# Opening of a diffusion-step kernel: PSUM banks by name, vec first on SyncE's queue, one gate product and two modulation products moved

## The chip, the cores and the metric

The kernel runs on one core of one Trainium2 chip. The metric is device microseconds of one execution, lower is better, as the median of three runs.

## The reference, cut to what matters

One layer of a hybrid backbone over 512 latent tokens ("sample", with their own state and conditioning) and 128 context tokens ("prompt"), width 1024, all in 32-bit floats.

```python
mod = silu(cond) @ w_ada + b_ada                      # 1024 x 3072
shift, scale, gate = split(mod, 3)
h = rmsnorm(x, norm_w) * (1 + scale) + shift
z = h @ w_in                                          # 1024 x 10752: q, k, v, g_ret, x_lru, g_lru, m_ret, m_lru
o = retention(q, k, v)                                # 4 heads, chunks of 128, both directions
ret_out = (groupnorm(o) * gn_w * silu(g_ret)) @ w_ret_down
xc = short_conv(x_lru)
r, i = sigmoid(xc_block @ wa + ba), sigmoid(xc_block @ wx + bx)    # 10 blocks of 128, both directions
hf, hb = scans of (exp(-8 r softplus(-a)), sqrt(1 - a^2) i xc)
lru_out = ((hf + hb) * silu(g_lru)) @ w_lru_down
y = rmsnorm(x + gate * ((sigmoid(m_ret) * ret_out + sigmoid(m_lru) * lru_out) @ w_out), final_norm_w)
```

The outputs are y of both groups and the final states of the prompt.

## The kernel before, in words

All 640 tokens are worked on together. Every large product takes its operands as a high and a low half, and `mm3` (L413) issues three matmuls for it: high by high (L414), high by low of the other operand (L415), low by high (L416). ScalarE makes a high half by a copy, VectorE the low half by a subtraction (L420). Halves are named h and l: hTh, hTl are the modulated, transposed input, yh, yl the retention output, sh, sl weights or sums of inputs.

**The opening** (L635 to L960). SyncE's queue (SP) loads the five x tiles (`load_x`), then the modulation weights (`load_ada`, four pieces of 256 KB for each block of 128 channels) and the first weights (`load_wf`). The vector of small parameters, pv, is loaded from ScalarE's queue. ScalarE squares each x tile (its output goes to the PSUM tile sq) and takes the root, VectorE scales the tile (`norm_x`). Meanwhile TensorE multiplies the identity with itself (`warm`, eight times at first and eight times behind each x tile).

Each of the eight channel blocks then needs: its transposes (`x_s` for the four sample tiles, `x_t` for the prompt tile), the copies out of PSUM (`ev_s`, `ev_p`), a modulation product of 1024 x 256 (`mod_mm`, L757), two one-column products that turn its result (`mod_cols`, L769, L770), two small VectorE operations that give the factors mA and mB, and `h_mod`, which applies them. With `both`, ScalarE writes hTh from the copy and VectorE makes the 32-bit values of its own; without, ScalarE does it all in three activations; hTl is VectorE's subtraction, last. Transposes go to three PSUM tiles of two banks each, taken in turn from one pool (`psz`); the prompt transposes of all eight blocks share one such tile and are copied out alternately by VectorE and ScalarE. Two further banks (mb) hold the modulation products.

The first three output blocks of w_in (`z_first(i, kt)`, six matmuls each) are then summed over the eight channel blocks in eight steps. Step kt also holds the modulation product and h_mod of block kt + 2, and the split of its first weights (`wf_high`, `wf_low`). All of this is written out in a fixed order for each engine. Behind step 7 come the next weights ("fm", NEXT) and the paired products with the sums (S1 to S4) that `sum_3` and `sum_124` make from blocks k and k + 4 on both engines.

**Work behind the opening** on ScalarE and VectorE is put in order by `Plan`: each piece is a generator with estimated costs and a rank (`prio`, lower goes first): 0.7 for the sums, 0.8 and more for weight splits (`ahead`, by how far ahead a weight stands), 1.3 for the evacuation of a gate product, more by 0.5 where the activation table must be changed. `feed` issues the next slab of the weight stream whenever one of four raw buffers is free; `stream_order` writes the order of that stream.

**Gate products** of the recurrent branch (`gates(j)`, L1199 on): four groups of two banks, 24 matmuls, each bank emptied by a sigmoid (L1212). `GATES_AT` names the place of each of the ten among the other products: "A" for the pairs, a head's number with a step of it, "D" for the sixteen pieces of the down product (`DOWN`). Product 7 stands behind the last head's attention, ("at"), ahead of the down piece (0, 0). A down piece keeps two banks over both its halves. Behind piece 0 stand two units of transposes of the last head (`y_unit`, L1568, two banks each), then piece 1. There are eight banks in all.

Of the kernel before, what the change touches and what calls it, by code (L numbers as in the profile page):

```python
# [8 lines left out]
F32 = mybir.dt.float32  # L9
# [34 lines left out]
def first_col(b):  # L44
# [4 lines left out]


GATES_AT = {("A", 10): 0, ("A", 20): 1, ("A", 26): 2, (0, "sc"): 3, (1, "v3"): 4, (1, "kv"): 5,
            (2, "sc"): 6, (3, "at"): 7, ("D", 5): 8, ("D", 9): 9}


def stream_order():
# [248 lines left out]
def tile_hybrid_step(  # L304
# [329 lines left out]
    def load_x(t):  # L634
        src = x_sample[128 * t:128 * t + 128, :] if t < 4 else x_prompt  # L635
        nc.sync.dma_start(out=xt[t], in_=src)
# [20 lines left out]
        dve0.tensor_tensor(lo[:, 0:384], wf_raw[kt], f32(hi[:, 0:384]), op=SUB)  # L657
        raws.give(wf_raw.pop(kt))

    load_x(0)  # L660
    nc.scalar.dma_start(out=pv, in_=vec)
    for t in range(1, 5):
        load_x(t)
    for kt in range(4):
        load_ada(kt)
# [60 lines left out]
        dve0.tensor_scalar(s8, sp[:, 0:20], -8.0, None, op0=MUL)  # L726

    mb = [psp.tile([128, 512], F32, tag=f"b{i}", name="b") for i in range(2)]
    zpool = tc.tile_pool(name="zp", bufs=3, space=bass.MemoryType.PSUM, reuse_waits="tile")
    zp = zpool.__enter__()  # L730

    def psz():
        return zp.tile([128, 2, 512], F32, tag="z", name="z")

    sq = psz()

    def warm(n):
        for _ in range(n):
            pe.matmul(out=mb[1][:, 384:512], lhsT=ident, rhs=ident, start=True, stop=True)  # L739
# [35 lines left out]
    fulls, ready = {}, {}  # L775
    groups = ((slice(0, 512), 1), (slice(512, 640), 0))

    def x_t(o, kt, t):
        pe.transpose(o, xt[t][:, 128 * kt:128 * kt + 128], ident)

    def x_s(kt, z):
        for t in range(4):
            x_t(z[:, kt % 2, 128 * t:128 * t + 128], kt, t)

    def ev_s(kt, z, eng=act0):
        if eng is act0:
            act0.activation(fulls[kt][:, 0:512], z[:, kt % 2], AF.Copy)
        else:
            dve0.tensor_copy(fulls[kt][:, 0:512], z[:, kt % 2])

    def ev_p(kt, eng):
        out, src = fulls[kt][:, 512:640], zpr[:, kt // 4, 128 * (kt % 4):128 * (kt % 4) + 128]
        if eng is act0:
            act0.activation(out, src, AF.Copy)
        else:
            dve0.tensor_copy(out, src)

    def h_mod(kt, both=False, between=None):
        full = fulls[kt]
        for c, g in groups:  # L800
            a, b = mA[:, kt, g:g + 1], mB[:, kt, g:g + 1]
            if both:
                act0.activation(hTh[:, kt, c], full[:, c], AF.Identity, scale=a, bias=b)
        for c, g in groups:
            a, b = mA[:, kt, g:g + 1], mB[:, kt, g:g + 1]
            if both:
                dve0.tensor_scalar(full[:, c], full[:, c], a, b, op0=MUL, op1=ADD)
            else:
                act0.activation(full[:, c], full[:, c], AF.Identity, scale=a, bias=b)
        if not both:  # L810
            act0.activation(hTh[:, kt], full, AF.Copy)
        if between:
            between()
        dve0.tensor_tensor(hTl[:, kt], full, f32(hTh[:, kt]), op=SUB)
        ready[kt] = S.clock["dve"]

# [57 lines left out]

    for t in range(5):
        norm_x(t)
        warm(8)
    for kt in range(8):
        fulls[kt] = wide("hf")
    z01, zpr = psz(), psz()  # L880
    x_s(0, z01)
    x_s(1, z01)
    ev_s(0, z01)
    wf_high(0)
    ev_s(1, z01, dve0)
    mod_mm(0, dve0)
    load_ada(4)
    wf_low(0)
    load_wf(4)
    for kt in range(8):  # L890
        x_t(zpr[:, kt // 4, 128 * (kt % 4):128 * (kt % 4) + 128], kt, 4)
    for kt in range(4):
        ev_p(kt, dve0)
        ev_p(kt + 4, act0)
    mod_cols(0)
    z23 = psz()
    x_s(2, z23)
    x_s(3, z23)
    z45 = psz()
    x_s(4, z45)  # L900
    x_s(5, z45)
    h_mod(0, True, lambda: ev_s(3, z23, dve0))
    ev_s(2, z23)
    ev_s(4, z45)
    ev_s(5, z45, dve0)
    mod_mm(1)
    z67 = psz()
    zq = [psz(), psz(), psz()]
    S.pe = 19000.0
    for e in S.clock:  # L910
        S.clock[e] = 20000.0
# [5 lines left out]
        S.pump(S.pe)  # L917

    z_first(0, 0)
    x_s(6, z67)  # L920
    x_s(7, z67)
    ev_s(6, z67)
    ev_s(7, z67, dve0)
    wf_high(1)
    wf_low(1)
    xtp.__exit__(None, None, None)
    ttp, tr = open_pool("ttp", "right")
    tts.add(tr, [f"tt{i}" for i in range(3)])
# [4 lines left out]
    for kt in range(8):  # L933
        if kt:
            z_first(0, kt)
        if kt == 0:
            mod_cols(1)
            h_mod(1, True)
        if kt < 6:
            mod_mm(kt + 2)  # L940
            wf_high(kt + 2)
        z_first(1, kt)
        if kt < 6:
            mod_cols(kt + 2)
            wf_low(kt + 2)
            h_mod(kt + 2)
        z_first(2, kt)
        slab.give(wf_hl.pop(kt))
        if kt < 3:
            load_ada(kt + 5)  # L950
            load_wf(kt + 5)
        else:
            feed()
        opened[0] = kt > 4
        if kt == 4:
            job(prep, "soft", prio=9.0)
        if kt in (0, 2):
            job(sum_3(kt), f"s3.{kt}", prio=0.7)
        if kt in (3, 5):
            k0 = kt - 3  # L960
            job(sum_124(k0), f"s124.{k0}", prio=0.7)
# [1082 lines left out]
```

## Time and profile before

| | |
|---|---|
| median of 3 runs | 995.78 us (995.7 to 995.81) |
| the profiled execution | 993.75 us |
| its span, first to last instruction | 992.0 us |
| mean granted clock of TensorE | 0.996 |
| busy, TensorE / VectorE / ScalarE | 98% / 74% / 55% |

A profile is of one execution. Times in its rows count from the start of the span. The releaser in brackets names what ended the idle time of the engine just ahead of an instruction. PE is TensorE, DVE VectorE, ACT ScalarE, SP SyncE. A clock of 1.00 is 2.4 GHz, 0.5 is 1.2 GHz.

### The profile page before, as it was taken

How to read it: one execution, taken by the hardware profiler on the slowest of the kernel's cores; microseconds unless marked ns; L12 is line 12 of the kernel's file. 1: busy time of each engine (PE TensorE's matmuls, PEld its weight loads, DVE VectorE, ACT ScalarE, POOL GpSimd, SP SyncE). 2: the span in 40 equal slices, each digit the busy share in tenths (PEclk: the TensorE clock that was granted, in tenths of full speed). 3: DMA queues.
4: the chain of work that ended last, by engine and by line, in shares of the span. 5: the costliest groups of instructions: out<-in, count | busy, mean ns of one | idle time of the engine just before them, and what ended most of it. 6: DMA issues, size and time to landing. Idle time of an engine off the chain costs nothing.

```text
span 992.0 us, 15489 instructions
## 1 busy us (share of the span) xinstructions
PE 976.1 (98%) x6061; PEld 916.7 (92%) x6061; DVE 733.2 (74%) x1137; ACT 542.5 (55%) x852; POOL 2.2 (0%) x13
## 2 busy tenths in 40 slices
PE   8999999999999999999999999999999999999997
PEld 7789999999999999999888888888789999999986
DVE  4699977679986799784676887886768878646554
ACT  6765454476555765663468597376575545324222
POOL 0000000000000000000000000000000000000000
PEclk9999999999999999999999999999999999999999
DMA  9644444433453334445533534454634555635312
GB/s 343 229 144 156 150 165 139 128 112 131 170 170 130 142 130 155 160 138 165 174 121 114 194 127 157 157 170 151 204 118 160 188 190 184 237 125 178 117 64 85
DMA packets 61015, 155.52 MB, mean 157 GB/s; under 512 B 6778, under 2 KB 9998, under 8 KB 60942
## 3 DMA queue, kind: packets, MB, share of 16 engines
q1 hardware_dynamic: 60654, 154.18, 46.3%
q8 instruction: 47, 0.77, 0.3%
q10 hardware_dynamic: 288, 0.36, 0.1%
q14 instruction: 26, 0.21, 0.1%
HBM read 118.20 MB, written 36.32 MB: 156 GB/s over the span
## 4 chain that ended last, share of the span: by engine, by line
PE 90%; DVE 5%; ACT 4%; DMA 1%; issue 1%; POOL 0%; DVEq 0%; POOLq 0%; ACTq 0%
PE z L414 29%; PE z L416 29%; PE z L415 29%; PE b L739 1%; ACT hf L294 1%; PE z L1568 1%; DVE sl L420 1%; ACT hTh L294 1%; DVE hTl L294 1%; DVE yl L420 0%; DMA y<-sg 0%; DVE hf L294 0%; DMA yf<-y 0%; ACT sh L539 0%; DVE xc L1177 0%
## 5 line engine op out<-in xcount | busy, mean ns | idle before, releaser
L420 DVE TENSOR_TENSOR sl<-raw,sh 128x1024 fp32r<-128x1024 f32 (+1 forms) x128 | 133.3, 1045 | 48.8 <-ACT sh L505 48.5
L505 ACT ACTIVATE sh<-raw 128x1024 fp32r<-128x1024 f32 (+1 forms) x96 | 96.9, 1013 | 127.0 <-PE z L415 81.7
L414 PE MATMUL z<-sh,sh 128*128 128x320 f32 x512 | 158.4, 309 | 0.8 <-ACT p L1038 0.8
L415 PE MATMUL z<-sl,sh 128*128 128x320 f32 x512 | 158.2, 309 | 0.0
L416 PE MATMUL z<-sh,sl 128*128 128x320 f32 x512 | 158.2, 309 | 0.0
L414 PE MATMUL z<-hTh,sh 128*128 128x320 f32 x432 | 134.8, 312 | 1.5 <-ACT hTh L294 1.5
L415 PE MATMUL z<-hTl,sh 128*128 128x320 f32 x432 | 133.7, 309 | 2.2 <-DVE hTl L294 2.2
L416 PE MATMUL z<-hTh,sl 128*128 128x320 f32 x432 | 133.5, 309 | 0.0
L414 PEld LDWEIGHTS z<-sh,sh 128*128 128x128 f32 x512 | 96.1, 188 | 1.3 <-ACT p L1038 1.3
L415 PEld LDWEIGHTS z<-sl,sh 128*128 128x128 f32 x512 | 96.1, 188 | 0.0
L416 PEld LDWEIGHTS z<-sh,sl 128*128 128x128 f32 x512 | 96.1, 188 | 0.0
L414 PEld LDWEIGHTS z<-hTh,sh 128*128 128x128 f32 x432 | 81.1, 188 | 4.7 <-issue 2.5
L415 PEld LDWEIGHTS z<-hTl,sh 128*128 128x128 f32 x432 | 81.1, 188 | 2.7 <-DVE hTl L294 2.7
L414 PE MATMUL z<-yh,sh 128*128 128x320 f32 x256 | 80.1, 313 | 2.3 <-ACT gt L1212 2.2
L416 PEld LDWEIGHTS z<-hTh,sl 128*128 128x128 f32 x432 | 81.1, 188 | 0.0
L415 PE MATMUL z<-yl,sh 128*128 128x320 f32 x256 | 79.8, 312 | 0.0
L416 PE MATMUL z<-yh,sl 128*128 128x320 f32 x256 | 79.8, 312 | 0.0
L414 PE MATMUL z<-sh,hTh 128*128 128x512 f32 x160 | 62.9, 393 | 0.0
L416 PE MATMUL z<-sh,hTl 128*128 128x512 f32 x160 | 62.4, 390 | 0.0
L415 PE MATMUL z<-sl,hTh 128*128 128x512 f32 x160 | 62.3, 389 | 0.0
L414 PEld LDWEIGHTS z<-yh,sh 128*128 128x128 f32 x256 | 48.6, 190 | 2.8 <-ACT gt L1212 2.5
L1085 ACT ACTIVATE p<-z 128x320 f32<-128x320 f32 x32 | 14.0, 438 | 67.3 <-PE z L416 67.3
(258 smaller groups left out, 2233.2 us busy)
## 6 DMA issues: line engine op xcount, KB each, us to landing
raw<-in_w_str_dram SPq DMA_DIRECT2D x131, 512.0 KB, 3.7
adr<-in_w_ada_dram SPq DMA_DIRECT2D x32, 256.0 KB, 5.6
g<-c SPq DMA_DIRECT2D x16, 320.0 KB, 2.2
sg<-g SPq DMA_DIRECT2D x16, 320.0 KB, 4.0
out_dram<-kv SPq DMA_DIRECT2D x16, 256.0 KB, 3.2
y<-sg SPq DMA_DIRECT2D x12, 320.0 KB, 2.2
yf<-y SPq DMA_DIRECT2D x12, 320.0 KB, 4.6
x<-c SPq DMA_DIRECT2D x10, 320.0 KB, 3.7
```

What stands on the lines that cost most here:

```text
L294: return f(*args, **kw)
L414: pe.matmul(out=out, lhsT=lh, rhs=rh, start=start, stop=False, **kw)
L415: pe.matmul(out=out, lhsT=lh, rhs=rl, start=False, stop=False, **kw)
L416: pe.matmul(out=out, lhsT=ll, rhs=rh, start=False, stop=stop, **kw)
L420: dve.tensor_tensor(out, full, f32(hi), op=SUB)
L505: act.activation(hi[:, 0:w], raw, AF.Copy)
L739: pe.matmul(out=mb[1][:, 384:512], lhsT=ident, rhs=ident, start=True, stop=True)
L1085: act.activation(self.tmp[:, 2], self.a[:, 0:H], AF.Copy)
L1568: pe.transpose(z[:, 128 * t:128 * t + 128] if t < 4 else zp_[:, 0:128], o[t][:, 128 * i:128 * i + 128], ident)
```

## The change

- Gate product 7, its weights in the stream and its wait for the block's convolution move from behind the attention of head 3 to behind the first down piece.
- pv is loaded on SP's queue, ahead of x, in place of ScalarE's queue behind x0. Warm-up products behind each x tile: six in place of eight.
- The three PSUM tiles get names z0, z1, z2. `x_T` makes all five transposes of a block in one of them (prompt in its second bank), and `x_out` copies them out on one engine. Block 0 and 1 come first, blocks 2 and 3 behind the column products of block 0, blocks 4 to 7 behind the first products of step 0 (before: 0 to 5 ahead of them). The three accumulators are z0, then z2 and z1, once blocks 6 and 7 are copied out.
- In `h_mod` with `both`, VectorE writes to a second buffer in place of the one that ScalarE reads.
- The column products and h_mod of block 1 move from step 0 to between the transposes of blocks 5 and 6. The modulation product of block 6 goes to the end of step 3, its columns and h_mod to step 4, and all of block 7 to step 4. Step 5 has neither any more.

```diff
@@ -49,7 +49,7 @@
 
 
 GATES_AT = {("A", 10): 0, ("A", 20): 1, ("A", 26): 2, (0, "sc"): 3, (1, "v3"): 4, (1, "kv"): 5,
-            (2, "sc"): 6, (3, "at"): 7, ("D", 5): 8, ("D", 9): 9}
+            (2, "sc"): 6, ("D", 0): 7, ("D", 5): 8, ("D", 9): 9}
 
 
 def stream_order():
@@ -657,9 +657,8 @@
         dve0.tensor_tensor(lo[:, 0:384], wf_raw[kt], f32(hi[:, 0:384]), op=SUB)
         raws.give(wf_raw.pop(kt))
 
-    load_x(0)
-    nc.scalar.dma_start(out=pv, in_=vec)
-    for t in range(1, 5):
+    nc.sync.dma_start(out=pv, in_=vec)
+    for t in range(5):
         load_x(t)
     for kt in range(4):
         load_ada(kt)
@@ -726,13 +725,13 @@
         dve0.tensor_scalar(s8, sp[:, 0:20], -8.0, None, op0=MUL)
 
     mb = [psp.tile([128, 512], F32, tag=f"b{i}", name="b") for i in range(2)]
-    zpool = tc.tile_pool(name="zp", bufs=3, space=bass.MemoryType.PSUM, reuse_waits="tile")
+    zpool = tc.tile_pool(name="zp", bufs=1, space=bass.MemoryType.PSUM, reuse_waits="tile")
     zp = zpool.__enter__()
 
-    def psz():
-        return zp.tile([128, 2, 512], F32, tag="z", name="z")
-
-    sq = psz()
+    def psz(i):
+        return zp.tile([128, 2, 512], F32, tag=f"z{i}", name="z")
+
+    sq = psz(2)
 
     def warm(n):
         for _ in range(n):
@@ -775,42 +774,39 @@
     fulls, ready = {}, {}
     groups = ((slice(0, 512), 1), (slice(512, 640), 0))
 
-    def x_t(o, kt, t):
-        pe.transpose(o, xt[t][:, 128 * kt:128 * kt + 128], ident)
-
-    def x_s(kt, z):
-        for t in range(4):
-            x_t(z[:, kt % 2, 128 * t:128 * t + 128], kt, t)
-
-    def ev_s(kt, z, eng=act0):
-        if eng is act0:
-            act0.activation(fulls[kt][:, 0:512], z[:, kt % 2], AF.Copy)
-        else:
-            dve0.tensor_copy(fulls[kt][:, 0:512], z[:, kt % 2])
-
-    def ev_p(kt, eng):
-        out, src = fulls[kt][:, 512:640], zpr[:, kt // 4, 128 * (kt % 4):128 * (kt % 4) + 128]
-        if eng is act0:
-            act0.activation(out, src, AF.Copy)
-        else:
-            dve0.tensor_copy(out, src)
-
-    def h_mod(kt, both=False, between=None):
-        full = fulls[kt]
+    def x_T(kt, i):
+        z = psz(i)
+        for t in range(5):
+            o = z[:, 1, 0:128] if t == 4 else z[:, 0, 128 * t:128 * t + 128]
+            pe.transpose(o, xt[t][:, 128 * kt:128 * kt + 128], ident)
+        return z
+
+    def x_out(kt, z, eng=act0):
+        fulls[kt] = full = wide("hf")
+        for c, src in ((groups[0][0], z[:, 0]), (groups[1][0], z[:, 1, 0:128])):
+            if eng is act0:
+                act0.activation(full[:, c], src, AF.Copy)
+            else:
+                dve0.tensor_copy(full[:, c], src)
+
+    def h_mod(kt, both=False):
+        raw = full = fulls[kt]
+        if both:
+            fulls[kt] = full = wide("hf")
         for c, g in groups:
             a, b = mA[:, kt, g:g + 1], mB[:, kt, g:g + 1]
             if both:
-                act0.activation(hTh[:, kt, c], full[:, c], AF.Identity, scale=a, bias=b)
+                act0.activation(hTh[:, kt, c], raw[:, c], AF.Identity, scale=a, bias=b)
         for c, g in groups:
             a, b = mA[:, kt, g:g + 1], mB[:, kt, g:g + 1]
             if both:
-                dve0.tensor_scalar(full[:, c], full[:, c], a, b, op0=MUL, op1=ADD)
+                dve0.tensor_scalar(full[:, c], raw[:, c], a, b, op0=MUL, op1=ADD)
             else:
                 act0.activation(full[:, c], full[:, c], AF.Identity, scale=a, bias=b)
         if not both:
             act0.activation(hTh[:, kt], full, AF.Copy)
-        if between:
-            between()
+        else:
+            W6.give(raw)
         dve0.tensor_tensor(hTl[:, kt], full, f32(hTh[:, kt]), op=SUB)
         ready[kt] = S.clock["dve"]
 
@@ -874,38 +870,23 @@
 
     for t in range(5):
         norm_x(t)
-        warm(8)
-    for kt in range(8):
-        fulls[kt] = wide("hf")
-    z01, zpr = psz(), psz()
-    x_s(0, z01)
-    x_s(1, z01)
-    ev_s(0, z01)
+        warm(6)
+    z = x_T(0, 0)
+    mod_mm(0, dve0)
+    x_out(0, z)
     wf_high(0)
-    ev_s(1, z01, dve0)
-    mod_mm(0, dve0)
     load_ada(4)
+    z = x_T(1, 1)
     wf_low(0)
     load_wf(4)
-    for kt in range(8):
-        x_t(zpr[:, kt // 4, 128 * (kt % 4):128 * (kt % 4) + 128], kt, 4)
-    for kt in range(4):
-        ev_p(kt, dve0)
-        ev_p(kt + 4, act0)
+    x_out(1, z)
     mod_cols(0)
-    z23 = psz()
-    x_s(2, z23)
-    x_s(3, z23)
-    z45 = psz()
-    x_s(4, z45)
-    x_s(5, z45)
-    h_mod(0, True, lambda: ev_s(3, z23, dve0))
-    ev_s(2, z23)
-    ev_s(4, z45)
-    ev_s(5, z45, dve0)
+    z2, z3 = x_T(2, 2), x_T(3, 1)
+    h_mod(0, True)
+    x_out(2, z2, dve0)
+    x_out(3, z3)
     mod_mm(1)
-    z67 = psz()
-    zq = [psz(), psz(), psz()]
+    zq = [psz(0), None, None]
     S.pe = 19000.0
     for e in S.clock:
         S.clock[e] = 20000.0
@@ -917,12 +898,17 @@
         S.pump(S.pe)
 
     z_first(0, 0)
-    x_s(6, z67)
-    x_s(7, z67)
-    ev_s(6, z67)
-    ev_s(7, z67, dve0)
+    z4, z5 = x_T(4, 2), x_T(5, 1)
+    x_out(4, z4)
+    x_out(5, z5, dve0)
+    mod_cols(1)
+    z6, z7 = x_T(6, 2), x_T(7, 1)
+    h_mod(1, True)
+    x_out(6, z6)
+    x_out(7, z7, dve0)
     wf_high(1)
     wf_low(1)
+    zq[1:] = [psz(2), psz(1)]
     xtp.__exit__(None, None, None)
     ttp, tr = open_pool("ttp", "right")
     tts.add(tr, [f"tt{i}" for i in range(3)])
@@ -933,18 +919,23 @@
     for kt in range(8):
         if kt:
             z_first(0, kt)
-        if kt == 0:
-            mod_cols(1)
-            h_mod(1, True)
+        if kt == 4:
+            mod_cols(6)
+            h_mod(6)
+        if kt < 5:
+            mod_mm(kt + 2 + (kt == 4))
         if kt < 6:
-            mod_mm(kt + 2)
             wf_high(kt + 2)
         z_first(1, kt)
+        if kt < 5:
+            mod_cols(kt + 2 + (kt == 4))
         if kt < 6:
-            mod_cols(kt + 2)
             wf_low(kt + 2)
-            h_mod(kt + 2)
+        if kt < 5:
+            h_mod(kt + 2 + (kt == 4))
         z_first(2, kt)
+        if kt == 3:
+            mod_mm(6)
         slab.give(wf_hl.pop(kt))
         if kt < 3:
             load_ada(kt + 5)
```

## Rows read from the trace of the kernel before

**Rows 1.** The profile page, busy time, share of the span and instructions by engine.
```profile
PE 976.1 (98%) x6061; PEld 916.7 (92%) x6061; DVE 733.2 (74%) x1137; ACT 542.5 (55%) x852; POOL 2.2 (0%) x13
```

**Rows 2.** Busy time by stretch: length, busy (instructions) by engine, PEclk, DMA share, GB/s.
```profile
18.20:22.40 4.20, 2.08 (x25) 1.03 (x22) 2.85 (x8) 2.52 (x6) 0.00 (x0) 1.00 1.01 374
...
58.00:68.60 10.60, 10.60 (x74) 10.60 (x73) 10.39 (x21) 8.21 (x12) 0.00 (x0) 1.00 0.44 159
```

**Rows 3.** DMA issues with size and time to landing, and two issues on SP.
```profile
g<-c SPq DMA_DIRECT2D x16, 320.0 KB, 2.2
...
0.74 0.39 SPq L636 DMA_DIRECT2D x<-in_x_sample_dram  x1
...
x<-in_x_sample_dram SPq DMA_DIRECT2D x1, 512.0 KB, 4.3
...
11.40 0.33 SPq L642 DMA_DIRECT2D adr<-in_w_ada_dram  x1
...
adr<-in_w_ada_dram SPq DMA_DIRECT2D x1, 256.0 KB, 6.0
```

**Rows 4.** Timeline, opening: start, length, engine, line, operation, [idle before <-releaser].
```profile
5.25 0.22 ACT L294 ACTIVATE cs<-pv 128x16 f32<-128x16 f32 x1 [2.80 <-DMA pv<-in_vec_dram]
...
7.32 1.01 ACT L294 ACTIVATE z<-x 128x1024 f32<-128x1024 f32 x1
...
14.48 0.75 DVE L294 TENSOR_SCALAR x<-x,rst 128x1024 f32<-128x1024 f32 x1
...
14.61 1.07 PE L757 MATMUL b<-adr,c 128*32 128x256 f32 x16
...
16.69 0.36 PE L770 MATMUL b<-pv,mod 128*128 128x2 f32 x2
...
18.65 0.29 DVE L294 COPY hf<-z 128x128 f32<-128x128 f32 x1 [0.34 <-ACT hf L294]
...
19.36 1.20 ACT L294 ACTIVATE hTh<-hf,mB,mA 128x512 fp32r<-128x512 f32 x2
...
21.52 0.81 DVE L294 TENSOR_TENSOR hTl<-hf,hTh 128x640 fp32r<-128x640 f32 x1
...
22.39 0.41 PE L415 MATMUL z<-hTl,sh 128*128 128x320 f32 x1 [1.75 <-DVE hTl L294]
...
29.38 0.31 PE L414 MATMUL z<-hTh,sh 128*128 128x320 f32 x1
```

**Rows 5.** Timeline, steps 5 to 7 and the next weights.
```profile
48.34 0.74 ACT L294 ACTIVATE hTh<-hf 128x640 fp32r<-128x640 f32 x1
...
54.74 0.41 PE L414 MATMUL z<-hTh,sh 128*128 128x320 f32 x1 [1.11 <-ACT hTh L294]
55.60 0.41 PE L415 MATMUL z<-hTl,sh 128*128 128x320 f32 x1 [0.45 <-DVE hTl L294]
...
58.19 0.31 PE L414 MATMUL b<-hTh,sh 128*128 128x320 f32 x1
```

**Rows 6.** Timeline and one stretch, from the attention's end to the second down piece.
```profile
723.65 3.77 DVE L420 TENSOR_TENSOR yl<-yf,yh 128x640 fp32r<-128x640 f32 x5
...
728.23 0.30 PE L414 MATMUL z<-xh,sh 128*128 128x320 f32 x1
...
734.12 0.41 PE L414 MATMUL z<-yh,sh 128*128 128x320 f32 x1 [2.21 <-ACT gt L1212]
...
735.00:738.40 3.40, 3.40 (x16) 3.40 (x15) 2.48 (x3) 3.40 (x8) 0.00 (x0) 0.54 0.18 30
...
743.80 0.40 PE L414 MATMUL z<-yh,sh 128*128 128x320 f32 x1
```

**Rows 7.** Timeline of ScalarE at gate product 8.
```profile
780.61 1.06 ACT L505 ACTIVATE sh<-raw 128x1024 fp32r<-128x1024 f32 x1 [5.93 <-PE z L415]
781.69 1.28 ACT L1212 ACT_TABLE_LOAD   x1
782.99 3.46 ACT L1212 ACTIVATE gt<-z,pv 128x320 f32<-128x320 f32 x8
```

## Prediction, before the change was run

> **What bounds the kernel now.** I read the page first: TensorE is busy for 98% of the span [rows 1], and most of the chain that ended last is its matmuls. Time can only be won where TensorE stands or runs on its lower clock, so the next view was busy time by stretch. Two places that the diff touches show idle TensorE. The first is the opening, from 0 to 58 us: between 18.2 and 22.4 us TensorE does 2.08 us of work in 4.20 [rows 2]. The second is the change from attention to the down product, at 732 us: a wait of 2.21 us, and behind it a stretch with a granted clock of 0.54 [rows 6]. Last I read single instructions at both places, to see what ends each wait.
>
> **Opening, before the first products.** In the trace of before the vector pv reaches ScalarE at 5.25; the squares of the five x tiles follow back to back from 7.32, 2.07 us later; the last tile is scaled at 14.48 + 0.75 = 15.23 [rows 4]. x0 is issued at 0.74 and takes 4.3 us, so it is there at 5.04 [rows 3]: ScalarE waits for pv, not for x. The change issues pv first on SP's queue, and what is moved behind it is every x tile, by one issue of about 0.4 us.
>
> Pv's transfer with nothing ahead of it is not in the trace. Bounds are 2.2 us (the fastest transfers of that size) and, with pv's arrival at 5.25, no gain at all [rows 3, 4]. I take 2.6, nearer the low end, since 98 KB are a fifth of x0. Then pv is there at 3.3, ScalarE is ready at 5.4, x0 lands at 5.45, and the squares begin at about 5.55: **1.75 us** earlier. The last x tile is scaled at 13.5.
>
> From there, with durations of rows 4: transposes of block 0 until 13.7, when modulation product 0 starts; its column products end 2.44 us after its start (14.61 to 16.69 + 0.36 before), at 16.1; the two small VectorE operations take 0.42 (from the end of the last copy to hTh), until 16.55; the hTh activations (1.20) until 17.85; hTl (0.81) until 18.7. Before, eight prompt copies that alternate between VectorE and ScalarE, each waiting for the other (the last: 0.34), stood ahead of this, about 2.5 us, and another block's copy stood ahead of hTl. The copies are now made with their own block, and a second buffer lets VectorE's hf run beside ScalarE's hTh.
>
> TensorE's order also has modulation product 1 ahead of the first products. Its last weights are issued at 11.40 and take 6.0 us [rows 3], so it can't end before 18.45; that edge lies 0.25 us inside the chain above and costs nothing. The product that needs hTl starts at about 18.75 in place of 22.39 [rows 4].
>
> Part is given back at once, because the named banks are now reused in a chain. Blocks 4 to 7 are transposed behind the first products, in two banks that must be emptied in turn; product (1, 0) waits until block 6 is copied out (about 24.3, a stand of 0.75 us), and (2, 0) until block 7 is (25.2). Step 1 starts at about 26.7 in place of 29.38 [rows 4]: **2.7 us** won.
>
> **Modulation products of blocks 6 and 7.** The number of products is the same. Removed: the two waits for hT(7), 1.11 + 0.45 = 1.56 us [rows 5]. Added: a wait in step 4. There the copy of product 7 stands on ScalarE behind all of h_mod(6): two hf activations (1.20 together) and one hTh (0.74) [rows 4, 5], which start only after mA(6). TensorE has product 7 (1.07 [rows 4]) and z(1, 4), about 2 us with their gaps, to cover this; then it waits at the column product of block 7 for about 0.9 us, or 1.7 if VectorE runs one sum of hTl's size (0.81) first. I take 1.3. Behind that wait stand z(2, 4) and all of steps 5 to 7. The next weights' first product would start at 58.19 - 2.7 - 1.6 + 1.3 = 55.2 [rows 5].
>
> This 3.0 us does not arrive whole. From 58.0 to 68.6 VectorE is busy 10.39 of 10.60 us [rows 2]: that stretch follows VectorE. Its work is the same, started 2.7 us earlier, less some 0.4 us more idle time in step 4, where no split fills VectorE's wait for hTh(6). I put the **opening at -2.3 us**. The bounds are 0 (all swallowed) and -3.4 (all passed on).
>
> **Gate product 7 behind the first down product.** Before, it starts at 728.23; TensorE then waits 2.21 us for ScalarE to empty a bank, because a square-root and then a sigmoid table stand ahead, and of the following 3.40 us at a clock of 0.54 some 1.56 us are lost: 3.8 us in all [rows 6]. After, the down product (0, 0) starts at 728.23. What it needs is there: its weights come one place earlier in the stream, two banks are free (the gate took two at the same moment), and the last low half of the y tiles ends at 723.65 + 3.77 = 727.42 [rows 6], a cover of 0.8 us. It takes 7.0 us (743.80 - 734.12, less the 1.56 and about 1.1 for the transposes), until 735.25.
>
> Then comes the gate, half as many matmuls and 3.5 us, with six banks, since the down product keeps two. The nearest rows are those of gate 8 at 780 us: a weight split of 1.06 that waits for the slab just released, a table load of 1.28, eight sigmoids in 3.46 [rows 7]. Put at 735.3, the sigmoids run from 737.7 to 741.15. The gate's last group waits 0.2 us for a bank, the two sets of transposes behind it wait for the next two pairs, and the second down product for the last pair, at 741.2. Before, it began at 743.80 [rows 6]. **Gain 2.6 us**; the bounds are 0 and 3.8. The chain of block 7 ends later, and gate 9 is the next that needs it, some 70 us on.
>
> The sigmoid of that row starts 0.02 us after the table load's end [rows 7], so the sum takes 1.28 for the switch. The Trainium skill (ScalarE: Activation LUTs, What ACT_TABLE_LOAD costs) puts a drain of about 1.38 us behind each such load; by it the gain here would be an estimated 1.2 us and the time 992.3.
>
> **Sum.** -2.3 - 2.6 = -4.9 us, against the profiled execution of 993.75 us (span 992.0). That stands 2.03 below the median of the runs, 995.78; taken from the median it gives **990.9**. A measurement of this kernel can tell about 0.2%, 2.0 us.
>
> **The rivals.**
> *Both gains whole.* VectorE's sums fit into its idle time, and the sigmoid table is loaded while the down product runs, so no bank is late: -3.4 - 3.8, 988.6. Against it: the same pattern at 780 us has split and load in sequence [rows 7]. Chance 0.11.
> *The hand-over swallows the opening.* VectorE, full from 58 us on [rows 2], orders its sums so that nothing is won there: -0.5 - 2.6, 992.7. Chance 0.13.
> *The opening loses the upper clock.* Ten of the 48 warm-up products go, so TensorE runs out of them and has only transposes until the last x tile is scaled at 13.5. After the stand of 2.21 us the granted clock was 0.54 [rows 6]; with 2.08 us of work in 4.20 it stayed at 1.00 [rows 2]. The case lies between. At half clock the transposes, column products and product 1 put the first products back by about 0.75 us: 991.7. Chance 0.10.
> The Trainium skill (TensorE: Matmul & The Clock Gate, HAM oscillation) warns that idle gaps between bursts throttle the array again; by that rule this case is the likely one.
> *The banks come late at the gate.* One more split (1.06) or table load (1.28) ahead of the sigmoids, and a lower clock after it: -2.3 - 0.5, 993.0. Chance 0.10.
> *The change does not do what it says.* Pv lands no earlier and its place in the queue costs x 0.4 us; the chain of named banks eats the rest; the gate's wait only moves: 995.4. Chance 0.07.
> *Slower.* The sums rank ahead of weight splits, and blocks 6 and 7 now release theirs earlier. If all of them (12 half-width sums at about 0.5 and six low halves of hTl's size, 0.81 [rows 4]: some 11 us of VectorE) run before the low half of the next weights, which TensorE took at 58.19 without a wait [rows 5], it ends near 62 and TensorE stands six microseconds at 55, then runs at half clock: the first product of these weights comes about 3 us later than 58.19, 1.6 us more go to the clock, 2.6 come back at the gate: 997.8. It turns slower once that low half ends after about 59. Against it: before, that split was ready in time with most of the sums still to come. Chance 0.09.
>
> **How the numbers follow.** The forecast has 0.40, with a range of its own of 989.7 to 992.1. Faster by over 0.2% (below 993.8): 0.40 + 0.10 + 0.11, most of the swallowed opening (0.10) and half of the late banks (0.05): 0.76. Within 0.2%: the rest of these (0.03 + 0.05) and the 0.07: 0.15. Slower: 0.09. From 988.2 to 995.2 leaves out about half of the first rival, half of the one that does nothing, and the slow one: 0.18.
>
> **What would show it.** Right: the first square near 5.6, the hTl product near 18.8, step 1 near 26.7; no wait for hTh in steps 6 and 7 and one of about 1 us in step 4, at the column product of block 7; the first product of the sums 2.3 us earlier than before. At the gate: no wait of over 1 us on a bank, the clock at 1.00, and the second down product 2.6 us earlier relative to the end of attention. Wrong: pv still reaching ScalarE near 5, no earlier start of the sums' first product, or a clock below 1 at 12 to 18 us or around 740.

## The result, and the profile after

The changed kernel takes **988.15 us** (median of 4 executions, 986.95 to 989.18), the kernel before 995.74 (4, 995.62 to 995.81) beside it on the same chip: a ratio of 0.9923, 95% interval [0.9906, 0.9941], some 7.6 us. The forecast was 990.9 with a range from 988.2, so the gain is 2.75 us larger than forecast, and the time lies just outside the range. The profiled execution of after took 988.05 (span 986.2); that of before took 993.75 (992.0). Between these two the gain is 5.7.

The page's busy times hardly change (compare [rows 1]): the work is the same, and less time is lost around it.

```profile
PE 974.7 (99%) x6041; PEld 915.3 (93%) x6041; DVE 732.5 (74%) x1135; ACT 542.7 (55%) x854; POOL 2.2 (0%) x13
```

The timeline of the opening, after; it answers to [rows 4].

```profile
2.64 0.21 ACT L294 ACTIVATE cs<-pv 128x16 f32<-128x16 f32 x1 [0.62 <-DMA pv<-in_vec_dram]
5.24 1.03 ACT L294 ACTIVATE z<-x 128x1024 f32<-128x1024 f32 x1 [0.44 <-DMA x<-in_x_sample_dram]
...
12.42 0.75 DVE L294 TENSOR_SCALAR x<-x,rst 128x1024 f32<-128x1024 f32 x1
...
17.51 0.82 DVE L294 TENSOR_TENSOR hTl<-hf,hTh 128x640 fp32r<-128x640 f32 x1 [0.49 <-ACT hTh L294]
...
18.39 0.42 PE L415 MATMUL z<-hTl,sh 128*128 128x320 f32 x1 [0.16 <-DVE hTl L294]
...
26.53 0.31 PE L414 MATMUL z<-hTh,sh 128*128 128x320 f32 x1
```

The first square now waits for x, not for pv (5.24; before 7.32), and the product that needs hTl starts at 18.39 in place of 22.39.

Step 4 and the next weights, ScalarE and TensorE of after, and one row of busy time by stretch. They answer to [rows 5].

```profile
43.51 1.20 ACT L294 ACTIVATE hf<-hf,mB,mA 128x512 f32<-128x512 f32 x2 [2.60 <-DVE mA L294]
44.74 0.74 ACT L294 ACTIVATE hTh<-hf 128x640 fp32r<-128x640 f32 x1
45.38 0.36 ACT L294 ACTIVATE mod<-b 128x256 f32<-128x256 f32 x1
...
45.80 0.38 PE L768 MATMUL b<-pv,mod 128*128 128x2 f32 x2 [2.16 <-ACT mod L294]
...
56.69 0.31 PE L414 MATMUL b<-hTh,sh 128*128 128x320 f32 x1
...
67.25 0.38 PE L414 MATMUL z<-sh,sh 128*128 128x320 f32 x1
```
```profile
46.30:49.70 3.40, 3.40 (x14) 3.40 (x15) 1.64 (x5) 2.84 (x5) 0.00 (x0) 0.50 0.37 90
```

The waits for hT(7) are gone. The copy of product 7 stands behind three activations of block 6, as forecast, and TensorE waits 2.16 us for it. Then it runs at a granted clock of 0.50, the lower of its two levels. The first product of the sums (67.25) comes 2.09 us earlier than before (69.34).

The end of attention, TensorE and ScalarE of after; it answers to [rows 6, 7].

```profile
725.65 0.30 PE L414 MATMUL z<-yh,sh 128*128 128x320 f32 x1
732.68 0.31 PE L414 MATMUL z<-xh,sh 128*128 128x320 f32 x1
...
735.69 0.42 PE L414 MATMUL z<-xh,sh 128*128 128x320 f32 x1 [0.20 <-ACT gt L1203]
...
738.07 0.41 PE L414 MATMUL z<-yh,sh 128*128 128x320 f32 x1
```
```profile
732.74 1.06 ACT L505 ACTIVATE sh<-raw 128x1024 fp32r<-128x1024 f32 x1 [3.27 <-PE z L415]
733.82 1.28 ACT L1203 ACT_TABLE_LOAD   x1
735.11 3.45 ACT L1203 ACTIVATE gt<-z,pv 128x320 f32<-128x320 f32 x8
```

Down piece 0, gate, second down piece: 12.42 us in place of 15.57 before. ScalarE repeats the pattern of gate 8 [rows 7], and the only wait on a bank is 0.20 us.

### The profile page after: what moved, and what is told of

Same layout as the page of the kernel before. It is cut to its first block, busy times and chain, and to the rows that moved or that the text cites. A ratio compares the mean times of both kernels' runs of the same rounds, so it can differ in the third digit from the quotient of the medians.

```text
span 986.2 us, 15467 instructions
## 1 busy us (share of the span) xinstructions
PE 974.7 (99%) x6041; PEld 915.3 (93%) x6041; DVE 732.5 (74%) x1135; ACT 542.7 (55%) x854; POOL 2.2 (0%) x13
## 4 chain that ended last, share of the span: by engine, by line
PE 94%; ACT 3%; DVE 2%; DMA 1%; issue 0%; SPq 0%; DVEq 0%; ACTq 0%
PE z L414 31%; PE z L416 30%; PE z L415 30%; PE z L1559 1%; ACT z L294 1%; ACT hTh L294 0%; ACT hf L294 0%; DMA x<-in_x_sample_dram 0%; DMA y<-sg 0%; DVE sl L420 0%; DMA yf<-y 0%; PE b L756 0%; DVE hTl L294 0%; PE b L414 0%; PE b L416 0%
## 5 line engine op out<-in xcount | busy, mean ns | idle before, releaser
L420 DVE TENSOR_TENSOR sl<-raw,sh 128x1024 fp32r<-128x1024 f32 (+1 forms) x128 | 133.4, 1045 | 50.4 <-ACT sh L505 49.6
L414 PE MATMUL z<-lth,sh 128*128 128x320 f32 x160 | 49.6, 310 | 0.0
```

Source lines behind the costliest of these rows:

```text
L414: pe.matmul(out=out, lhsT=lh, rhs=rh, start=start, stop=False, **kw)
L420: dve.tensor_tensor(out, full, f32(hi), op=SUB)
```

## The experiments

**One part at a time.** The first question was where the missing 2 us are: in the change, or in the profiled execution of before, which is 2 us faster than the median of that kernel. Beside the runs of this group, before took 995.87 (23 executions, 993.75 to 997.45).

The kernel before, unaltered. 

> The kernel before, unchanged. Theory A: its ordinary executions (995.7 us) carry a second stretch at half clock that its profiled execution (993.75 us) escaped. One such stretch of 3.4 us costs about 1.7 us and lowers the mean granted clock by about 0.0017; so executions near 995.7 show a mean clock of about 0.994, and those near 993.7 one of 0.996. Theory B: the 2 us are lost elsewhere (outside the span, or a little everywhere): the mean clock is 0.996 in executions at 993.7 and at 995.7 alike.

It took 996.29 (993.66 to 997.29), its profiled execution 996.35. Start and length of all warm-up products, the hTl product, one stretch at half clock, and the next weights, of this execution:

```profile
1.36 13.30 PE L739 MATMUL b<-ident 128*128 128x128 f32 x96 [1.36 <-POOL ident masks.py:199]
...
23.25 0.60 PE L415 MATMUL z<-hTl,sh 128*128 128x320 f32 x1 [1.76 <-DVE hTl L294]
...
60.58 0.31 PE L414 MATMUL b<-hTh,sh 128*128 128x320 f32 x1
```
```profile
23.30:26.70 3.40, 3.40 (x15) 3.36 (x16) 0.69 (x1) 0.60 (x3) 0.00 (x0) 0.50 1.03 356
```

In the execution that the prediction was read from, the same row is shorter; the second line is the sums' first product, for later:

```profile
1.36 12.37 PE L739 MATMUL b<-ident 128*128 128x128 f32 x96 [1.36 <-POOL ident masks.py:199]
...
69.34 0.42 PE L414 MATMUL z<-sh,sh 128*128 128x320 f32 x1 [0.42 <-ACT p L1038]
```

The 48 products start at 1.36 in both and end at 13.73 or 14.66, by how early TensorE gets faster. From 4 to 6 us it ran 19 instructions in the execution of the prediction and 11 in this one (the clock's column shows 1.00 in both, so the rise is read from the counts):

```profile
4.00:6.00 2.00, 2.00 (x19) 2.00 (x18) 0.68 (x4) 0.53 (x3) 0.00 (x0) 1.00 1.02 411
...
4.00:6.00 2.00, 2.00 (x11) 2.00 (x10) 0.98 (x7) 0.90 (x3) 0.00 (x0) 1.00 1.05 407
```

The products stand on TensorE's queue ahead of the first transposes, so the hTl product comes 0.86 us later (22.39, 23.25), although the first square came 0.37 us earlier (7.32, 6.95). After a stretch at half clock, right behind the hTl product, the next weights start 2.39 later (58.19, 60.58). That is most of the difference between this execution and the one of the prediction (996.35, 993.75). The mean granted clock doesn't show it, against theory A: it is 0.996 in both. But that mean also counts the end of the span, where TensorE has nothing left to do and the clock was at 0.50 for 4.6 us in the one and for 1.8 us in the other:

```profile
987.33:991.90 4.57, 0.00 (x0) 0.00 (x0) 0.65 (x2) 1.11 (x3) 0.00 (x0) 0.50 0.30 115
...
992.70:994.50 1.80, 0.00 (x0) 0.00 (x0) 0.00 (x0) 0.00 (x0) 0.00 (x0) 0.50 0.31 120
```

The gate's edit alone: before, with `GATES_AT` and nothing else changed.

```diff
-            (2, "sc"): 6, (3, "at"): 7, ("D", 5): 8, ("D", 9): 9}
+            (2, "sc"): 6, ("D", 0): 7, ("D", 5): 8, ("D", 9): 9}
```

> Before with gate product 7 moved alone. The profiles of before and after put 3.1 us on this part (attention's end to the second down piece, 15.6 against 12.4 us); the prediction said 2.6. Theory A, with the second half-clock stretch in the opening: 995.7 - 3.1 = 992.6. If the second stretch lies at the gate, theory A gives 995.7 - 3.1 - 1.7 = 990.9. Theory B: 992.6.

992.48 (992.05 to 994.47), ratio 0.9971 [0.9962, 0.998]: 3.4 us less than before.

The opening alone: the changed kernel with that line put back.

> After with gate product 7 back behind the attention: the opening alone, with the moved modulation products. The profiles put 2.6 us on it (start of the piece behind the attention, 728.2 against 725.6). Theory A with the second stretch in the opening: 995.7 - 2.6 - 1.7 = 991.4; with it at the gate: 993.1. Theory B: 993.1.

991.52 (988.95 to 992.95), ratio 0.9956 [0.994, 0.9973]: 4.4 us less. The two add up to 7.8, the whole gain (7.6) within the noise. The gate was near its forecast, the opening was not.

The changed kernel with the modulation products of blocks 6 and 7 in steps 4 and 5 again.

```diff
-        if kt < 5:
-            mod_mm(kt + 2 + (kt == 4))
         if kt < 6:
+            mod_mm(kt + 2)
             wf_high(kt + 2)
```

> After with the modulation products of blocks 6 and 7 back in steps 4 and 5. It takes away the wait of 2.16 us in step 4 and the half-clock stretch behind it (1.6 us) and brings back the waits for hT(7), 1.6 us. Theory of the prediction, the hand-over to the sums follows VectorE: the sums' first product starts within 0.5 us of where it does in after (67.25), and the time is 988.2 within 0.7. Rival, TensorE's time in the steps is passed on whole: the sums start 2 us earlier and the time is near 986.0. Second rival, the moved products are worth what the waits say (1.6 us and more): 989.8 or above.

987.55 (987.14 to 990.13), ratio 0.992 [0.9904, 0.9936]. Moving these products is worth nothing that can be measured. Its profiled execution, the slowest (990.13), shows the rival in which the opening loses the upper clock:

```profile
14.50:21.20 6.70, 6.70 (x47) 4.47 (x39) 3.72 (x9) 3.49 (x9) 0.00 (x0) 0.50 1.05 397
```

The hTl product came at 21.61 there, 3.2 us later than in after; the rival had put 0.75. So this profile can't tell where the sums would start without the moved products, and that part of the expectation stays open.

**The parts of the opening** (before, beside these runs: 996.26, 14 executions). Before with 6 warm-up products behind each x tile in place of 8, nothing else.

> The kernel before with 6 warm-up products in place of 8 behind each x tile (38 in all), nothing else changed. Theory A (the two microseconds that the forecast missed lie in the opening: in before the 48 warm-up products end later than the last x tile is scaled whenever the clock rises late, 12.4 to 13.9 us in three executions, so most executions lose about 1 to 1.5 us there that the profiled one did not): 38 products end near 11 us, ahead of the last scaled tile, the product that needs hTl starts at 22.2 to 22.5 whatever the rise, and the median is 1 to 2 us below that of before, 993.8 to 994.8. Rival B (the number of warm-up products has nothing to do with it): the median stays within 0.4 us of before, near 995.8, and the hTl product moves with the rise of the clock. Rival C (the clock falls in the opening with fewer products): a half-clock stretch between 12 and 22 us and a median of 996.5 or more.

994.17 (992.05 to 995.98), ratio 0.998 [0.997, 0.9991]: 2.1 us (0.9 to 3.0 by the interval) from one digit that the prediction had costed at nothing, and theory A's time. Warm-up products, transposes and hTl product, and a stretch at half clock behind it:

```profile
1.36 10.62 PE L739 MATMUL b<-ident 128*128 128x128 f32 x76 [1.36 <-POOL ident masks.py:199]
...
13.54 0.77 PE L779 MATMUL z<-ident,x 128*128 128x128 f32 x5 [1.04 <-DVE x L294]
...
22.02 0.41 PE L415 MATMUL z<-hTl,sh 128*128 128x320 f32 x1 [1.76 <-DVE hTl L294]
```
```profile
22.40:25.70 3.30, 3.30 (x17) 3.26 (x15) 0.68 (x1) 0.73 (x3) 0.00 (x0) 0.50 1.05 384
```

The products end at 11.98, and TensorE then waits for an x tile: their length no longer sets anything. From the first square to the hTl product it took 15.08 us here and 15.07 in the execution of the prediction, where the queue was hidden too, but 16.30 in the repeat of before and 16.72 in the run with the gate's edit alone. So the queue cost the profiled executions 0 to 1.6 us. The stretch at half clock is not prevented: it is here as in the repeat, and this execution (995.49) is slower than its median. How the 2.1 us divide between the queue and such stretches is not shown.

The reverse: the changed kernel with `warm(8)`.

> The changed kernel with 8 warm-up products behind each x tile again (48 in all). Theory A: they end at 12.4 to 13.9 us, about as late as the last x tile is scaled (13.2) or up to 0.7 later, so the hTl product comes at 18.4 to 19.2 and the median rises by 0.5 to 1.0 us, to 988.7 to 989.2. Rival B (the queue of warm-up products is hidden): 988.15 within 0.4. Rival C (fewer products cost the clock): the median falls by 0.5 us or more, below 987.6, and the clock stays up from 12 to 50 us.

989.21 (988.0 to 991.0), ratio 0.9936 [0.9923, 0.9949], by medians 1.1 us slower than after as first measured. The products ran until 14.56, 1.7 us past the last scaled tile (12.83), and all behind them came later, by more than theory A had, which took the lengths of 12.4 to 13.9 us for ends (they start at 1.36):

```profile
1.36 13.20 PE L738 MATMUL b<-ident 128*128 128x128 f32 x96 [1.36 <-POOL ident masks.py:199]
...
19.94 0.41 PE L415 MATMUL z<-hTl,sh 128*128 128x320 f32 x1 [0.17 <-DVE hTl L294]
```

The changed kernel with pv on ScalarE's queue behind x0, as before.

> The changed kernel with the vector pv back where it was: on ScalarE's queue, behind x0 on SP's. Theory A (pv's arrival starts the chain of the opening, and all of it reaches the first products): the first square starts near 7.3 in place of 5.24, the last x tile is scaled near 15.2, the hTl product starts at 20.2 to 20.5 in place of 18.39, and as VectorE sets the hand-over only part arrives: a median of 989.2 to 990.2. Rival B (the named banks and not pv won the opening): the hTl product within 0.5 us of 18.4 and 988.2. Rival C (whole): 990.3 or more.

991.38 (989.37 to 993.74), ratio 0.9956 [0.9941, 0.9972]: 3.2 us slower, rival C by its time. The chain moved by only 1.68 us (hTl product at 20.07). Means of the granted clock are 0.991 to 0.996 over the six executions, against 0.994 to 0.999 of after. TensorE stands a little longer for the last x tile than in after (1.04 us, there 0.80):

```profile
14.90 0.33 PE L782 MATMUL z<-ident,x 128*128 128x128 f32 x1 [1.04 <-DVE x L294]
...
20.07 0.42 PE L415 MATMUL z<-hTl,sh 128*128 128x320 f32 x1 [0.16 <-DVE hTl L294]
```

So pv's place is worth 1.7 us of the chain; the other 1.5 us are open. The lower means point to the clock, but the profiled execution (989.59, the second fastest of the six) has it at 1.00 all through the opening and one stretch at 0.50, in step 4, as after has. Nor do fewer warm-up products cost the clock whenever pv comes late: before with six had means of 0.994 to 0.998, before with eight 0.992 to 0.997.

Before with both edits, pv first and `warm(6)`, and the old banks (before 996.11, 13 executions).

> The kernel before with two of the change's edits: pv first on SP's queue and 6 warm-up products behind each x tile; banks, modulation products and gate as before. Theory A (pv's arrival moves the whole chain of the opening, as the changed kernel with pv moved back showed): the first square near 5.3, the hTl product near 20.1, and a median 1.5 to 2.5 us below that of 6 warm-up products alone (994.2), so 991.7 to 992.7; the rest of the opening's gain, 0.2 to 1.2 us, is the banks'. Rival B (the eight prompt copies of the old banks set the opening): the hTl product at 21 or later and a median of 993.5 or more.

993.5 (991.46 to 994.29), ratio 0.9971 [0.996, 0.9982]: rival B by its numbers, but not by its reason. Pv adds only some 0.7 us to six products alone, and the two intervals overlap. The first square came 1.72 us earlier than there (5.22, 6.94), the hTl product 0.69 (21.33, 22.02). The eight prompt copies don't make the difference: from the first of them to the hTl product it is 5.65 us here and 5.64 there. The time goes ahead of them, where modulation product 0 takes 2.09 us in place of 1.07, because two pieces of its weights have not landed when it starts. Weight loads of TensorE, first prompt copy, hTl product:

```profile
13.34 0.14 PEld L756 LDWEIGHTS b<-adr,c 128*32 128x32 f32 x4 [0.48 <-DMA adr<-in_w_ada_dram]
13.99 0.14 PEld L756 LDWEIGHTS b<-adr,c 128*32 128x32 f32 x4 [0.51 <-DMA adr<-in_w_ada_dram]
...
15.68 0.29 DVE L294 COPY hf<-z 128x128 f32<-128x128 f32 x1
...
21.33 0.41 PE L415 MATMUL z<-hTl,sh 128*128 128x320 f32 x1 [1.75 <-DVE hTl L294]
```

From the same first square (5.22; 5.24 in after) the changed kernel has this product at 18.39. So the banks, with their new order of copies and the second buffer, are worth 2.9 us there.

**The wait in step 4.** The changed kernel with the product of block 7 ahead of `h_mod(6)`, so that its copy is not behind that block's activations.

```diff
         if kt == 4:
             mod_cols(6)
+            mod_mm(7)
             h_mod(6)
-        if kt < 5:
-            mod_mm(kt + 2 + (kt == 4))
+        if kt < 4:
+            mod_mm(kt + 2)
```

> The changed kernel with product 7 of the modulation ahead of h_mod(6) in step 4, so that its copy on ScalarE no longer stands behind the two hf activations and the hTh copy of block 6. Theory A (the hand-over follows VectorE, so TensorE's time here isn't passed on): the wait of 2.16 us for the copy at 45.8 and the half-clock stretch behind it go, the next weights' first product comes 0 to 2 us earlier than 56.69, the first product of the sums moves by less than 0.7 from 67.25, and the median by less than 0.5 from 988.15. Rival B (TensorE's time is passed on): 2.2 us of wait and about 1.6 us of clock come back, 984.5 to 986.

990.25 (989.27 to 991.15), ratio 0.9943 [0.9931, 0.9955]: neither theory; it got slower by 2.1 us. The wait is gone and the next weights start at 54.23, but TensorE now waits three times, 4.34 us in all. VectorE and TensorE:

```profile
51.15 0.56 DVE L294 TENSOR_TENSOR sl<-wfr,sh 128x384 fp32r<-128x384 f32 x1
...
54.68 1.22 DVE L420 TENSOR_TENSOR sl<-raw,sh 128x1024 fp32r<-128x1024 f32 x1
```
```profile
51.76 0.42 PE L416 MATMUL z<-hTh,sl 128*128 128x320 f32 x1 [1.31 <-DVE sl L294]
55.95 0.42 PE L416 MATMUL b<-hTh,sl 128*128 128x320 f32 x1 [1.27 <-DVE sl L420]
68.25 0.53 PE L414 MATMUL z<-sh,sh 128*128 128x320 f32 x1 [1.76 <-ACT p L1030]
```

VectorE comes to the last low half of step 7 at 51.15, only 0.6 us earlier than in after, and TensorE is there first. The sums start at 68.25 in place of 67.25, and behind the last of these waits a stretch at a granted clock of 0.50 follows, from 68.4 to 71.8. But the edit changed more than the place of one product: from 50.4 us on `Plan` has VectorE's work in another order. Nine more of the small operations come ahead of the low half of the next weights, which runs at 54.68, where after has it at 53.14. With after's own order the sums started at 66.28 without these waits, in the next profile of after. So this run doesn't show that the other engines hold TensorE back; it shows the cost of another order.

Next, the changed kernel again, and with warm-up products that fill the wait in place of removing it.

```diff
+        if kt == 4:
+            warm(18, 0)
         if kt < 5:
             mod_cols(kt + 2 + (kt == 4))
```

> The changed kernel unaltered, for the spread of its executions and as the mate of the next two. Theory A (a stretch at half clock costs its own time wherever it falls, and the executions differ by how many there are): a median of 987.6 to 988.8, with executions at a mean clock of 0.998 near 987.0 and those at 0.995 or 0.996 at 988 to 989.2. Rival B (the stretch in step 4 is swallowed by the hand-over): no difference in time between executions of clock 0.998 and 0.996.

> The changed kernel with 18 warm-up products (some 1.9 us at the upper clock) put into TensorE's wait of 2.16 us in step 4, ahead of the column products of block 7; they add nothing to the result. Theory A (the half-clock stretch of 3.4 us behind that wait costs its 1.7 us in full): the granted clock stays 1.00 from 42 to 70 us, the next weights' first product starts near 55.0 in place of 56.7, and the median falls by 1.0 to 1.7 us against the changed kernel of the same call. Rival B (VectorE sets the hand-over): the clock stays up as well, but new waits of about 1.7 us for low halves or p stand between 50 and 68 us, and the median stays within 0.5 us. Rival C: the stretch at half clock only comes later, and the median is up to 2 us higher, as with product 7's copy first.

After: 987.25 (986.61 to 990.48), ratio 0.9919 [0.9903, 0.9935]. With 18 products: 988.43 (988.13 to 988.84), ratio 0.9924 [0.9912, 0.9937]. The filler was mis-sized: 18 products (two instructions each in the trace) took 4.29 us, not 1.9, and outlasted the wait by 2 us.

```profile
44.07 4.29 PE L738 MATMUL b<-ident 128*128 128x128 f32 x36
```

It still tells something. The next weights started 2.01 us later than in the profiled execution of after beside it (57.43, 55.42; 0.26 of it was there at the hTl product), and the execution took 2.2 us longer (988.84, 986.63), with the clock at 0.999: a delay of TensorE here is paid in full, VectorE's work does not swallow it. That execution of after has the same wait of 2.15 us but no stretch at half clock:

```profile
46.30:49.70 3.40, 3.40 (x25) 3.40 (x25) 1.64 (x5) 3.11 (x6) 0.00 (x0) 1.00 0.28 61
```
```profile
46.07 0.38 PE L768 MATMUL b<-pv,mod 128*128 128x2 f32 x2 [2.15 <-ACT mod L294]
...
55.42 0.31 PE L414 MATMUL b<-hTh,sh 128*128 128x320 f32 x1
...
66.28 0.41 PE L414 MATMUL z<-sh,sh 128*128 128x320 f32 x1
```

The same filler with 7 warm-up products behind each x tile.

> The changed kernel with the 18 warm-up products in step 4 and 7 in place of 6 behind each x tile (43 in all), to fill TensorE's wait of 0.8 us for the last x tiles without outlasting it. Theory A: they end at 11.4 to 12.6 us, ahead of the last scaled tile (13.2), the hTl product stays at 18.4 to 18.7, stretches at half clock in the opening become rarer, and the median is 0 to 0.7 us below that of the step 4 filler alone, 986.3 to 987.0. Rival B: as with 8 behind each tile, the opening comes 0.5 to 1.5 us later and the median is above that of the step 4 filler alone by that much.

989.1 (988.72 to 989.54), ratio 0.9931 [0.9918, 0.9943]: 0.7 us above the filler alone, though the hTl product was not late (18.62): rival B by its time, but not by its place, and this is not explained.

Last, 8 products in place of 18, and the changed kernel beside it (before 995.86, 9 executions).

> The changed kernel with 8 warm-up products (1.9 us by the 0.24 us that each took) in TensorE's wait of 2.16 us in step 4; they add nothing to the result. Theory A (the half-clock stretch behind that wait is paid in full where it falls): the clock stays 1.00 from 42 us on, the next weights' first product comes 37.0 us or less behind the hTl product, as in the execution without such a stretch (36.8), and the median is 986.5 to 987.0 with a spread under 1 us. Rival B (swallowed by VectorE's work): new waits before the sums and a median within 0.3 us of the changed kernel's in the same call.

> The changed kernel unaltered, as the mate of the one with 8 warm-up products in step 4: a median of 987.2 to 988.3, with executions from 986.6 to 990.5, by both theories.

With 8: 987.38 (986.64 to 988.8), ratio 0.9918 [0.9903, 0.9933]. After: 986.89 (986.68 to 989.06), ratio 0.9919 [0.9905, 0.9932]. Filler, column product and next weights:

```profile
43.95 2.05 PE L738 MATMUL b<-ident 128*128 128x128 f32 x16
46.23 0.38 PE L768 MATMUL b<-pv,mod 128*128 128x2 f32 x2 [0.22 <-ACT mod L294]
...
55.57 0.31 PE L414 MATMUL b<-hTh,sh 128*128 128x320 f32 x1
```

The clock stayed up in the profiled execution, and the mean is 0.998 in all five; the next weights come 36.76 us behind the hTl product, as theory A had it. Without a filler this distance was 36.76 in the execution with no stretch at half clock, 38.30 with one (the first profile of after), and 39.73 in the one profiled here, where it was longer:

```profile
45.90:52.70 6.80, 6.80 (x28) 6.80 (x29) 4.54 (x13) 3.17 (x6) 0.00 (x0) 0.53 0.27 77
```

So a stretch is paid nearly in full: 1.54 us for 3.4 us at half clock, 2.97 for 6.8. But the median is no lower than that of after, and the spread is 2.2 us where theory A had under 1: two executions at a clock of 0.998 took 988.1 and 988.8, by something else. This version, after, and the one with the products in their own steps can't be told apart; no version that was run beats the changed kernel.

## Why the prediction was wrong, step by step

**Opening, up to the first products: right.** First square 5.24 (forecast 5.55), last x tile scaled 13.17 (13.5), hTl done 18.33 (18.7), its product 18.39 (18.75), step 1 at 26.53 (26.7). Everything is 0.2 to 0.4 us early. Pv came sooner than I put (used at 2.64; 3.3), even below my bound, which was read from transfers of another size; but the first square waits for x, and that was there 0.2 us sooner (5.24; 5.45).

**Wait in step 4: right in place and cause, low in size.** 2.16 us; I had 1.3 with a bound of 1.7. mA(6), which ScalarE's three activations wait for, came 1.5 us behind its column product, because VectorE ran a low half and two sums first (from 41.41 to 43.1), where I allowed for one operation. Not foreseen was the stretch at half clock behind it, 1.5 us in the profiled execution.

**Hand-over to the sums: the size was off.** I let VectorE take 0.7 of 3.0 us. With no stretch at half clock the next weights start at 55.42 (forecast 55.2) and the sums at 66.28, 3.06 us earlier than before (69.34); with one it was 2.09. The delay put in by the filler arrived whole too. Whether VectorE would bound it from the other side, were TensorE freed of its wait in step 4, is open, since the run that tried it also changed VectorE's order.

**Gate: right, 0.5 us short.** -3.15 in the profiles and -3.4 alone, against -2.6. The down piece took 7.03 us (7.0), and split, table and sigmoids came as in [rows 7]. The failing term is the last: I let the second down piece wait for the last pair of banks, 13.0 us behind the end of attention; it started at 12.42, ahead of the end of the sigmoids, and on the upper clock.

The sigmoids began 0.01 us after the table load's end (733.82 + 1.28, 735.11). The Trainium skill's drain of 1.38 us behind each load (ScalarE: Activation LUTs, What ACT_TABLE_LOAD costs) is not seen in this trace either; the gain by it would have been an estimated 1.2 us.

**The sum: the step that failed.** It is the base: "taken from the median it gives" 990.9. I worked out -4.9 against an execution of 993.75 and took it from a median of 995.78, as if the 2 us between them would be there after the change as before. They are not a constant. The 75 executions of before in all runs together go from 993.57 to 997.53 with a median of 995.95, so the profiled one was near the best: two were faster. Against its own base the sum was 0.8 us off (988.85; the profiled execution of after took 988.05); the other 1.9 us or so of the miss are the base. The two other executions of the old opening with 48 products that were profiled pay for a late rise of the clock through that queue (1.2 and 1.6 us from the first square to the hTl product) and for a half-clock stretch behind it. The changed kernel's 38 products end ahead of the last scaled x tile in the first profile of after and at worst 0.1 us behind it (12.92, 12.81, in the fastest one). The prediction saw these ten products only as a risk to the clock and never asked what waits behind them. Alone they are worth 2.1 us, the opening as a whole 4.4 in place of 2.3.

The first rival (both gains whole, 988.6) came nearest, in part by luck: part of the gain came from the warm-up queue, which it did not name, and at the gate its mechanism did not occur, since the table was loaded at 733.82, behind the down piece. The lower clock in the opening, which the prediction also calls the likely case, stands in one of the nine profiles that have six warm-up products and pv first (the one with the products in their own steps). The slow rival did not occur in after: no wait for the next weights' low half stands in its profile. It did where product 7 went ahead of `h_mod(6)`, with 1.27 us.

Open: between the sums and the end of attention the kernels with the gate moved take 657.98 to 658.67 us (659.64 with product 7 ahead of `h_mod(6)`, which has a stretch at half clock there), those without 658.64 to 659.77. I found no single wait that explains these few tenths.

## What to carry to other kernels

Before a gain is taken from a median, ask what sets the profiled execution apart from it, with two or three more profiles of the same kernel: a spread of 4 us is itself a cost, and a change can remove it. A fixed number of warm-up products is work at the head of TensorE's queue whose length depends on when the clock rises; it should end before its cover does, even where the clock rises late. What is brought forward ends at the next thing that is not there yet: with pv early in the old opening, 1.0 of 1.7 us went to weights still on their way. And where a planner orders the other engines' work, compare their order before and after an edit: moving one product ahead in step 4 reordered VectorE's list, and TensorE stood twice as long.

## What was not expected of the hardware

The same wait (2.15 or 2.16 us, in the same place) was followed by the upper clock in one execution, by one stretch at half clock in the next, and by one of twice that length in a third. The times of the changed kernel fall into groups that fit it, though only these three were profiled: of 15 executions, seven at a mean clock of 0.998 or 0.999 took 986.6 to 987.0, five at 0.996 took 987.9 to 988.5, three at 0.994 or 0.995 took 989.1 to 990.5.

The Trainium skill (TensorE: Matmul & The Clock Gate, The HAM clock gate) says that the rise at a kernel's start varies from run to run with the phase of the gate. The traces agree that it varies: the 48 warm-up products of before took 12.37, 13.30 and, in the run with the gate's edit alone, 13.91 us (what it varies with, no run here shows):

```profile
1.36 13.91 PE L739 MATMUL b<-ident 128*128 128x128 f32 x96 [1.36 <-POOL ident masks.py:199]
```
